# RMSNorm with swish on one core: regrouped loads and stores, a held first store, more row sums on ScalarE, and a small transfer ahead of gamma's

## The chip, the cores and the metric

The kernel runs on one NeuronCore of a Trainium2 chip. The metric is the device time of one launch in microseconds (us). A profiled execution also gives a span, from the first to the last instruction on the core.

## What is computed

The input `x` is 16 x 1024 x 512 in float32, that is 16384 rows of 512 numbers, 33.55 MB; the output has the same size. The reference, cut to what matters:

```python
rms = np.sqrt(np.mean(x ** 2, axis=-1, keepdims=True) + eps)
x_norm = x / rms * gamma
return x_norm * (1.0 / (1.0 + np.exp(-x_norm)))
```

So each row needs one sum of squares, one reciprocal square root, a product with gamma and the swish of the result.

## The kernel before, in words

**Tiles.** The 16384 rows are 128 per row of the tile, one or more for each of the 128 partitions. `sizes` cuts the 128 rows that each partition holds into 11 tiles of 4, 4, 8, six of 16, 8 and 8 rows. One row in one partition is 2 KB, so a tile of 16 rows is 4 MB, and in HBM each partition's part of it is one piece of 32 KB. `xb` is a ring of 96 rows in SBUF: tiles 0 to 7 fit without waiting, while the last three tiles overwrite the places of earlier ones and their loads wait until those are stored. Everything happens in place in `xb`.

**Loads.** All 11 loads are issued by SyncE (L118), the first two from the very start of the program. SyncE waits on the store's semaphore `st` where a load overwrites the ring.

**Units.** The work goes in 32 units of `cn` = 4 rows of each partition. For unit k:

- ScalarE, `square(k)`: waits for the tile's load at its first unit; one ACTIVATE squares the last row and adds it up into `ms` (L159, followed by a read of the accumulator); a second one squares the other three rows (`n_sq` = 3) into the PSUM buffer `sq[k % 2]` (L166), which waits for the sums of unit k - 2.
- VectorE, `sums(k)` (L204): one TENSOR_REDUCE of the three squared rows.
- GpSimd: adds eps (L141) and raises to -0.5 (L148), giving `rstd`.
- VectorE, `norm(k)` (L215): four SCALAR_TENSOR_TENSOR, one for each row, times `rstd` and gamma.
- ScalarE, `swish(k)` (L178): one ACTIVATE over the four rows.

**Order by hand.** Every engine takes its instructions in the written order. ScalarE: `square(k)`, then a store that has become due, then `swish(k - 2)`. VectorE: `sums(k)`, then `norm(k - 1)`. Once, between `sums(0)` and `sums(1)`, VectorE spreads gamma over the partitions with a STREAM_SHUFFLE (L228), which waits for gamma's load.

**Stores.** ScalarE issues them (L183) on its own DMA queue, each as soon as the last unit of its tile has its swish. The same queue carries gamma's load, 8 KB, as its first transfer (L187), after GpSimd has set `gamma4` to zero (L136). Gamma's load is followed on ScalarE by the load of the activation table (L190).

At the end SyncE waits for the stores that no load waited for. In the trace the queue q1 is SyncE's (loads) and q10 is ScalarE's (gamma and stores).

Of the kernel before, what the change touches and what calls it, by code (L numbers as in the profile page):

```python
# [8 lines left out]
@with_exitstack  # L9
def kernel(  # L10
    ctx: ExitStack,
    tc: tile.TileContext,
    x: bass.AP,
    gamma: bass.AP,
    eps: bass.AP,
    out: bass.AP,
):
    nc = tc.nc
    P = nc.NUM_PARTITIONS
    AF = mybir.ActivationFunctionType  # L20
    ALU = mybir.AluOpType
    fp32 = mybir.dt.float32
    bf16 = mybir.dt.bfloat16

    xf = x.flatten_outer_dims()
    of = out.flatten_outer_dims()
    R, D = xf.shape


    sizes = [4, 4, 8] + [16] * 6 + [8, 8]  # L30
    ring = 96
    early = 2
    cn = 4
    n_sq = 3
    N = sum(sizes)
    assert N * P == R, (N, R)


    tiles = []
    done = 0  # L40
    for sz in sizes:
        assert done % ring + sz <= ring
        tiles.append((done * P, sz, done % ring))
        done += sz
    T = len(tiles)

    chunks = [
        (t, r, r == at)
        for t, (_, sz, at) in enumerate(tiles)
        for r in range(at, at + sz, cn)  # L50
    ]
    K = len(chunks)
    ends = []
    e = 0
    for sz in sizes:
        e += sz // cn
        ends.append(e)

    inv_d = 1.0 / float(D)
    eps_f = float(eps)  # L60

    tc.close()
    tc.compile()  # L65

    def sbuf(name, shape, dt=fp32):
        return nc.alloc_sbuf_tensor(name, shape, dt).ap()

    xb = sbuf("xb", [P, ring, D])  # L70
    gamma4 = sbuf("gamma4", [P, D])
    gamma_sb = sbuf("gamma_sb", [P, D])
    junk = [sbuf(f"junk{i}", [P, D], bf16) for i in range(2)]
    neg_half = sbuf("neg_half", [P, cn])
    ms = sbuf("ms", [P, K, cn])
    aeps = sbuf("aeps", [P, K, cn])
    rstd = sbuf("rstd", [P, K, cn])
    sq = [nc.alloc_psum_tensor(f"sq{i}", [P, 4, D], fp32).ap() for i in range(2)]

    ld = [nc.alloc_semaphore(f"ld{t}") for t in range(T)]  # L80
    st = [nc.alloc_semaphore(f"st{t}") for t in range(T)]
    s_gld = nc.alloc_semaphore("s_gld")
    s_zero = nc.alloc_semaphore("s_zero")
    s_half = nc.alloc_semaphore("s_half")
    s_gamma = nc.alloc_semaphore("s_gamma")
    s_acc = nc.alloc_semaphore("s_acc")
    s_sq = nc.alloc_semaphore("s_sq")
    s_sum = nc.alloc_semaphore("s_sum")
    s_eps = nc.alloc_semaphore("s_eps")
    s_rstd = nc.alloc_semaphore("s_rstd")  # L90
    s_norm = nc.alloc_semaphore("s_norm")
    s_swish = nc.alloc_semaphore("s_swish")

    def need(ins, sem, value):
        return ins.wait_op(sem, value, "sem-ge")

    def dram(ap, t):
        first, sz, _ = tiles[t]
        return ap[first : first + P * sz].rearrange("(p n) d -> p n d", n=sz)

    def buf(t):
        _, sz, at = tiles[t]
        return xb[:, at : at + sz, :]


    stored_by_sync = set()

    def load(t):
        _, sz, at = tiles[t]
        waits = [  # L110
            u for u in range(t)
            if tiles[u][2] < at + sz and at < tiles[u][2] + tiles[u][1]
            and u not in stored_by_sync
        ]
        for u in waits:
            nc.sync.wait_ge(st[u], 16)
            stored_by_sync.add(u)
        return nc.sync.dma_start(out=buf(t), in_=dram(xf, t)).then_inc(ld[t], 16)  # L118

    entry = nc.main_func.blocks[0].instructions  # L120
    here = nc.cur_bb.bb.instructions
    for t in range(early):
        ins = load(t).ins
        assert here[-1] is ins or here[-1].name == ins.name
        here.pop()
        at = next(
            i for i, other in enumerate(entry)
            if other.engine == mybir.EngineType.SP
            and isinstance(other, mybir.InstDrain)
        )  # L130
        entry.insert(at, ins)
    for t in range(early, T):
        load(t)


    nc.gpsimd.memset(gamma4, 0.0).then_inc(s_zero, 1)  # L136
    nc.gpsimd.memset(neg_half, -0.5).then_inc(s_half, 1)  # L137
    nc.gpsimd.wait_ge(s_half, 1)
    for k in range(K):
        need(  # L140
            nc.gpsimd.tensor_scalar(  # L141
                out=aeps[:, k, :], in0=ms[:, k, :], scalar1=eps_f, scalar2=None,
                op0=ALU.add,
            ),
            s_sum, k + 1,
        ).then_inc(s_eps, 1)
        need(
            nc.gpsimd.tensor_tensor(  # L148
                out=rstd[:, k, :], in0=aeps[:, k, :], in1=neg_half, op=ALU.pow
            ),  # L150
            s_eps, k + 1,
        ).then_inc(s_rstd, 1)


    def square(k):
        t, at, first = chunks[k]
        if first:
            nc.scalar.wait_ge(ld[t], 16)  # L158
        acc = nc.scalar.activation(  # L159
            out=junk[k % 2], in_=xb[:, at + n_sq, :], func=AF.Square,  # L160
            scale=inv_d**0.5, accum_out=ms[:, k, n_sq : n_sq + 1],
        )
        if k >= 2:
            need(acc, s_acc, k - 1)
        acc.then_inc(s_acc, 1)
        square = nc.scalar.activation(  # L166
            out=sq[k % 2][:, 0:n_sq, :], in_=xb[:, at : at + n_sq, :],
            func=AF.Square, scale=inv_d**0.5,
        )
        if k >= 2:  # L170
            need(square, s_sum, k - 1)
        square.then_inc(s_sq, 1)

    def swish(k):
        _, at, _ = chunks[k]
        rows = xb[:, at : at + cn, :]
        need(
            nc.scalar.activation(out=rows, in_=rows, func=AF.Silu), s_norm, k + 1  # L178
        ).then_inc(s_swish, 1)

    def store(t):
        need(
            nc.scalar.dma_start(out=dram(of, t), in_=buf(t)), s_swish, ends[t]  # L183
        ).then_inc(st[t], 16)

    need(
        nc.scalar.dma_start(out=gamma4[0:P:32, :], in_=gamma.partition_broadcast(4)),  # L187
        s_zero, 1,
    ).then_inc(s_gld, 16)
    nc.scalar.preload_act_table_set("silu_and_others")  # L190
    stored = 0
    for k in range(K + 3):
        if k < K:
            square(k)
        while stored < T and ends[stored] <= k - 2:
            store(stored)
            stored += 1
        if 2 <= k < K + 2:
            swish(k - 2)


    def sums(k):
        need(
            nc.vector.tensor_reduce(  # L204
                out=ms[:, k, 0:n_sq], in_=sq[k % 2][:, 0:n_sq, :], op=ALU.add,
                axis=mybir.AxisListType.X,
            ),
            s_sq, k + 1,
        ).then_inc(s_sum, 1)

    def norm(k):
        _, at, _ = chunks[k]
        for j in range(cn):
            row = xb[:, at + j, :]
            ins = nc.vector.scalar_tensor_tensor(  # L215
                out=row, in0=row, scalar=rstd[:, k, j : j + 1], in1=gamma_sb,
                op0=ALU.mult, op1=ALU.mult,
            )
            if j == 0:
                need(ins, s_rstd, k + 1)  # L220
        ins.then_inc(s_norm, 1)

    for k in range(K + 1):
        if k < K:
            sums(k)
        if k == 0:
            need(
                nc.vector.stream_shuffle(gamma_sb, gamma4, [0] * 32), s_gld, 16  # L228
            ).then_inc(s_gamma, 1)
        if k == 1:  # L230
            nc.vector.wait_ge(s_gamma, 1)
        if k >= 1:
            norm(k - 1)


    for t in range(T):
        if t not in stored_by_sync:
            nc.sync.wait_ge(st[t], 16)

# [34 lines left out]
```

## Time and profile before

| what | value |
|---|---|
| median of 12 runs | 160.25 us (160.15 to 160.34) |
| the profiled execution's own time | 160.15 us |
| its span | 158.8 us |
| VectorE busy | 139.2 us (88% of the span) |
| ScalarE busy | 125.1 us (79%) |
| GpSimd busy | 85.1 us (54%) |
| bytes moved | 67.14 MB, mean 423 GB/s |
| loads, 11 DMAs from SyncE | issued from 0.0 to 80.5 us |
| stores, 11 DMAs from ScalarE | issued from 16.26 to 152.17 us |

How to read it: the profiled execution took 160.15 us, of which 158.8 us lie between the first and the last instruction and 1.35 us around them; it stands 0.10 us under the median. An engine's busy time leaves out the issuing of DMAs and waits. The 16 DMA engines have a row of their own in the page: their mean busy share and what they moved in each of 40 slices. A DMA is split over these engines by partition, eight partitions each, and the trace has one packet for each piece of contiguous bytes in one partition: 8 KB for a tile of 4 rows, 16 KB for 8, 32 KB for 16. A group's mean time in the page is that of one instruction including what overlaps the next one; the distance between two starts in the timeline is the cost in a queue that is full.

### The profile page before, as it was taken

Reading aid. Unit: us, or ns where it says so; the run is one execution under the profiler, and the core shown is the slowest. Engines: PE = TensorE matmul, PEld = TensorE weight load, DVE = VectorE, ACT = ScalarE, POOL = GpSimd, SP = SyncE. Lnnn points to the kernel's source line nnn. Section 1 sums busy time; section 2 is a strip of 40 time slices with the busy share of each in tenths; the row PEclk is TensorE's granted clock in tenths of the full one; section 3 lists DMA queues with packets and bytes.
Section 4 is the critical chain, followed back from the end, with each engine's and each line's share of the span. In section 5 each row is a group of like instructions: output and inputs, shape, how many; then the busy total and the mean of one; then the engine's idle time right before and its main releaser. Section 6 shows DMA issues by size and latency. Waiting matters only on the chain.

```text
span 158.8 us, 437 instructions
## 1 busy us (share of the span) xinstructions
DVE 139.2 (88%) x162; ACT 125.1 (79%) x129; POOL 85.1 (54%) x70
## 2 busy tenths in 40 slices
DVE  0298986999999999999999999999999999998600
ACT  1838839888888899888888888899888888883430
POOL 1043551445555554444444557888888888988100
DMA  7999989989999989999999999999999999999997
GB/s 248 435 508 396 396 363 485 448 378 462 390 452 413 487 375 489 404 404 479 429 413 406 495 413 404 425 437 462 400 458 404 446 425 454 429 421 446 396 404 330
DMA packets 3179, 67.14 MB, mean 423 GB/s; under 512 B 356, under 2 KB 356, under 8 KB 360
## 3 DMA queue, kind: packets, MB, share of 16 engines
q1 hardware_dynamic: 1584, 33.56, 49.9%
q10 hardware_dynamic: 1592, 33.56, 49.2%
q14 instruction: 3, 0.02, 0.0%
HBM read 33.56 MB, written 33.55 MB: 423 GB/s over the span
## 4 chain that ended last, share of the span: by engine, by line
DVE 76%; DMA 13%; ACT 2%; POOL 2%; issue 0%; SPq 0%; ACTq 0%
DVE xb L215 47%; DVE ms L204 29%; DMA xb<-in_x_dram 13%; POOL aeps L141 2%; ACT xb L178 1%; ACT sq L166 1%; POOL rstd L148 1%; ACT junk L159 0%; SPq L118 0%; ACTq L158 0%
## 5 line engine op out<-in xcount | busy, mean ns | idle before, releaser
L215 DVE SCALAR_TENSOR_TENSOR xb<-xb,rstd,gamma_sb 128x512 f32<-128x512 f32 x128 | 87.8, 759 | 1.2 <-POOL rstd L148 1.2
L141 POOL TENSOR_SCALAR aeps<-ms 128x4 f32<-128x4 f32 x32 | 44.5, 1390 | 58.0 <-DVE ms L204 58.0
L178 ACT ACTIVATE xb<-xb 128x2048 f32<-128x2048 f32 x32 | 61.1, 1908 | 17.6 <-DVE xb L215 17.6
L204 DVE TENSOR_REDUCE ms<-sq 128x3 f32<-128x1536 f32 x32 | 56.5, 1765 | 9.8 <-ACT sq L166 9.7
L166 ACT ACTIVATE sq<-xb 128x1536 f32<-128x1536 f32 x32 | 45.9, 1434 | 0.0
L148 POOL TENSOR_TENSOR rstd<-aeps,neg_half 128x4 f32<-128x4 f32 x32 | 39.8, 1245 | 2.7
L159 ACT ACTIVATE junk<-xb 128x512 bf16<-128x512 f32 x32 | 19.7, 615 | 5.8 <-DMA xb<-in_x_dram 5.8
L159 ACT ACTIVATION_READ_ACCUMULATOR junk<-xb 128x1 f32 x32 | 6.0, 187 | 0.0
L190 ACT ACT_TABLE_LOAD x1 | 1.3, 1283 | 3.6 <-issue 3.6
L136 POOL MEMSET gamma<- 128x512 f32 x1 | 0.5, 524 | 1.5 <-POOLq L65 1.5
L228 DVE STREAM_SHUFFLE gamma_sb<-gamma 128x512 f32<-128x512 f32 x1 | 0.7, 720 | 0.0
L255 POOL MEMSET const-float32-0.0<- 128x1 f32 x1 | 0.1, 98 | 0.2 <-issue 0.2
L255 POOL MEMSET const-uint8-127<- 128x1 uint8 x1 | 0.1, 102 | 0.0
L255 POOL MEMSET const-bfloat16-1.0<- 128x1 bf16 x1 | 0.1, 101 | 0.0
L137 POOL MEMSET neg_half<- 128x4 f32 x1 | 0.1, 101 | 0.0
L255 POOL MEMSET const-float32-1.0<- 128x1 f32 x1 | 0.1, 98 | 0.0
L228 DVE LOAD_MASK_SELECT gamma_sb<-gamma x1 | 0.0, 14 | 0.0
## 6 DMA issues: line engine op xcount, KB each, us to landing
xb<-in_x_dram SPq DMA_DIRECT2D x6, 4096.0 KB, 43.5
out_dram<-xb ACTq DMA_DIRECT2D x6, 4096.0 KB, 29.8
xb<-in_x_dram SPq DMA_DIRECT2D x3, 2048.0 KB, 37.2
out_dram<-xb ACTq DMA_DIRECT2D x3, 2048.0 KB, 10.1
xb<-in_x_dram SPq DMA_DIRECT2D x2, 1024.0 KB, 5.9
out_dram<-xb ACTq DMA_DIRECT2D x2, 1024.0 KB, 19.5
gamma<-in_gamma_dram ACTq DMA_DIRECT2D x1, 8.0 KB
```

The source lines that it names most:

```text
L136: nc.gpsimd.memset(gamma4, 0.0).then_inc(s_zero, 1)
L137: nc.gpsimd.memset(neg_half, -0.5).then_inc(s_half, 1)
L141: nc.gpsimd.tensor_scalar(out=aeps[:, k, :], in0=ms[:, k, :], scalar1=eps_f, scalar2=None, op0=ALU.add,),
L148: nc.gpsimd.tensor_tensor(out=rstd[:, k, :], in0=aeps[:, k, :], in1=neg_half, op=ALU.pow),
L159: acc = nc.scalar.activation(out=junk[k % 2], in_=xb[:, at + n_sq, :], func=AF.Square, scale=inv_d**0.5, accum_out=ms[:, k, n_sq : n_sq + 1],)
L166: square = nc.scalar.activation(out=sq[k % 2][:, 0:n_sq, :], in_=xb[:, at : at + n_sq, :], func=AF.Square, scale=inv_d**0.5,)
L178: nc.scalar.activation(out=rows, in_=rows, func=AF.Silu), s_norm, k + 1
L190: nc.scalar.preload_act_table_set("silu_and_others")
L204: nc.vector.tensor_reduce(out=ms[:, k, 0:n_sq], in_=sq[k % 2][:, 0:n_sq, :], op=ALU.add, axis=mybir.AxisListType.X,),
L215: ins = nc.vector.scalar_tensor_tensor(out=row, in0=row, scalar=rstd[:, k, j : j + 1], in1=gamma_sb, op0=ALU.mult, op1=ALU.mult,)
L228: nc.vector.stream_shuffle(gamma_sb, gamma4, [0] * 32), s_gld, 16
L255: nc = _bacc.Bacc("TRN2", target_bir_lowering=False, num_devices=1)
```

## The change

Four things change together.

1. **A transfer of 8 KB out.** GpSimd first sets a tile `blank` of 128 x 16 floats to zero; ScalarE issues a DMA from it to a scratch tensor in HBM, ahead of gamma's on the same queue. It consists of 128 pieces of 64 bytes. SyncE waits for its end after its last load.
2. **Groups, loads and stores.** The tiles are replaced by five groups of 16, 48, 32, 16 and 16 rows, each contiguous in HBM. Loads and stores are pieces of a group. There are 8 loads in place of 11, two of them of 32 rows (64 KB in a partition), and 8 stores in place of 11, one of them of 32 rows. A load waits for whichever stores cover the rows that it overwrites: the load of group 3 for the store of group 0, the load of group 4 for the store of 32 rows.
3. **Held stores.** No store is issued before `square(8)` has been; before, the first one followed `square(3)`.
4. **Two row sums on ScalarE.** In every third unit (k % 3 == 2, ten units of the 32) ScalarE sums two rows with its accumulator and squares two for VectorE's reduction, in place of one and three. The accumulator's throw-away output alternates by row, with a semaphore for each buffer.

The loops of VectorE, of ScalarE and of GpSimd keep their order otherwise. The diff, cut to its core:

```diff
-    sizes = [4, 4, 8] + [16] * 6 + [8, 8]
+    groups = [16, 48, 32, 16, 16]
     ring = 96
+    loads = [(0, 0, 4), (0, 4, 4), (0, 8, 8), (1, 0, 16), (1, 16, 32), (2, 0, 32),
+        (3, 0, 16), (4, 0, 16)]
+    stores = [(0, 0, 16), (1, 0, 32), (1, 32, 16), (2, 0, 16), (2, 16, 16), (3, 0, 16),
+        (4, 0, 8), (4, 8, 8)]
-    n_sq = 3
+    held = 8
+    def n_sq(k):
+        return 2 if k % 3 == 2 else 3
...
+    ends = [-(-(begin[g] + r + n) // cn) for g, r, n in stores]
...
+    scratch = nc.dram_tensor("scratch", [P, 16], fp32, kind="Internal").ap()
+    blank = sbuf("blank", [P, 16])
...
     def dram(ap, piece):
+        g, r, n = piece
+        rows = ap[begin[g] * P : (begin[g] + groups[g]) * P]
+        return rows.rearrange("(p n) d -> p n d", n=groups[g])[:, r : r + n, :]
...
+    nc.sync.wait_ge(s_scratch, 16)
+    nc.gpsimd.memset(blank, 0.0).then_inc(s_blank, 1)
     nc.gpsimd.memset(gamma4, 0.0).then_inc(s_zero, 1)
...
     def square(k):
-        if first:
-            nc.scalar.wait_ge(ld[t], 16)
+        at, landing = chunks[k]
+        for i in landing:
+            nc.scalar.wait_ge(ld[i], 16)
+        n = n_sq(k)
+        for j in range(n, cn):
+            acc = nc.scalar.activation(
+                out=junk[j % 2], in_=xb[:, at + j, :], func=AF.Square,
+                scale=inv_d**0.5, accum_out=ms[:, k, j : j + 1],
+            )
...
+    need(nc.scalar.dma_start(out=scratch, in_=blank), s_blank, 1).then_inc(
+        s_scratch, 16
+    )
     need(
         nc.scalar.dma_start(out=gamma4[0:P:32, :], in_=gamma.partition_broadcast(4)),
         s_zero, 1,
     ).then_inc(s_gld, 16)
...
-        while stored < T and ends[stored] <= k - 2:
+        while k >= held and stored < len(stores) and ends[stored] <= k - 2:
             store(stored)
             stored += 1
...
-                out=ms[:, k, 0:n_sq], in_=sq[k % 2][:, 0:n_sq, :], op=ALU.add,
+                out=ms[:, k, 0 : n_sq(k)], in_=sq[k % 2][:, 0 : n_sq(k), :], op=ALU.add,
```

## The prediction

> **What bounds the kernel now.** I read the page first: engines, DMA row, queues.
>
> ```profile
> DVE 139.2 (88%) x162; ACT 125.1 (79%) x129; POOL 85.1 (54%) x70
> ...
> DMA  7999989989999989999999999999999999999997
> ...
> q1 hardware_dynamic: 1584, 33.56, 49.9%
> q10 hardware_dynamic: 1592, 33.56, 49.2%
> ```
>
> The two queues together use 99.1% of 16 engines' span: 157.4 of 158.8 us. The DMA engines are full from the first packet (0.99 us) to the last slice. The chain of waits nevertheless shows VectorE:
>
> ```profile
> 137.59 1.67 DVE ms L204
> 139.26 2.65 DVE xb L215 x4
> 141.91 1.68 DVE ms L204
> ...
> 147.46 2.75 DVE xb L215 x4
> 150.21 0.02 issue
> 150.23 1.91 ACT xb L178
> ```
>
> One unit costs VectorE 1.67 + 2.65 = 4.32 us, without a gap from unit 4 on. Both are true: the last store is issued at 152.17, its first packet starts at 153.01, and by the packet records the store ahead of it ends at 153.6. Compute is 0.6 us earlier than the DMA engines need it. The kernel is balanced, so a gain on one side alone is worth nothing. The timeline of one late unit shows ScalarE's part:
>
> ```profile
> 139.44 0.61 ACT L159 ACTIVATE junk<-xb 128x512 bf16<-128x512 f32 x1
> 140.05 1.43 ACT L166 ACTIVATE sq<-xb 128x1536 f32<-128x1536 f32 x1
> 141.78 1.79 DVE L204 TENSOR_REDUCE ms<-sq 128x3 f32<-128x1536 f32 x1
> 141.94 1.91 ACT L178 ACTIVATE xb<-xb 128x2048 f32<-128x2048 f32 x1 [0.45 <-DVE xb L215]
> ```
>
> The squares are ready at 141.48, 0.30 us before VectorE takes them: ScalarE has little room either.
>
> [...] with stores of 8 KB against loads of 32 KB the stores get 23% of the packet time from 20 to 24 us, near 8/(8+32). [...] Here a 32 KB packet takes 1213 ns, so 16 engines reach 432. Nothing in the change lifts that. [...] In the trace the eps addition takes 0.66 us up to 91.9 us and 2.65 us, the length of a norm, from 96.2 us on.
>
> **Part 1, fewer and longer packets.** Packets of 8, 16 and 32 KB take 309, 611 and 1213 ns: 2 x 309 - 611 = 7 and 2 x 611 - 1213 = 9, so about 8 ns for each packet beside its bytes. 22 DMAs with 8 packets per engine become 16: 48 fewer, -0.38 us; six completion packets of 9 ns less, -0.05. If rows of 64 KB travel as two packets, 24 of the 48 come back and the gain is 0.2. The rows of a group now lie 32 to 96 KB apart; I price that at nothing, as no row of before shows a cost.
>
> **Part 2, the scratch transfer.** Eight packets of 64 bytes per engine, unknown here: at least the 9 ns of a 4-byte packet, at most the 84 ns that gamma's 2 KB took, 0.07 to 0.67 us. I take 0.25. Besides, the first store has a price in before: from 18.8 us on, loads of 1213 ns took up to 1871, about 0.5 us on each engine, some 2.5 us after that store's issue:
>
> ```profile
> 16.00:20.00 4.00, 4.00 (x6) 3.31 (x5) 2.04 (x2) 1.00 1.03 393
> 20.00:42.00 22.00, 19.84 (x25) 17.97 (x20) 10.00 (x10) 1.00 0.99 423
> 42.00:70.00 28.00, 28.00 (x32) 24.83 (x26) 12.49 (x13) 1.00 1.01 435
> ```
>
> (Third to last column is the clock, then DMA share and GB/s: 393 against 435.) If it is a first write's cost, scratch pays it at 4 to 7 us instead; the engines are full there too, so it moves and is not saved: 0, with -0.5 as the other end. SP's added wait stands behind its last load and holds nothing up. On ScalarE the issue of gamma, the table load and unit 0 are queued behind scratch's: a first issue took 1.09 us (gamma, in before), a later one 0.34, so unit 0 starts at most 0.4 later than 4.87. The waits for loads ahead of units 1 and 2, 0.43 and 2.91 us, cover that; without them it would cost 0.4. GpSimd's added memset, 0.1 us, delays gamma's by as much.
>
> Gamma is behind scratch, and VectorE's shuffle behind gamma:
>
> ```profile
> 2.45 1.09 ACTq L187 DMA_DIRECT2D gamma<-in_gamma_dram  x1
> ...
> 8.65 0.72 DVE L228 STREAM_SHUFFLE gamma_sb<-gamma 128x512 f32<-128x512 f32 x1
> 9.45 1.76 DVE L204 TENSOR_REDUCE ms<-sq 128x3 f32<-128x1536 f32 x1
> ```
>
> Gamma's packet started at 7.42 and its completion was recorded at 8.58, just in time. Scratch is issued about 0.4 us earlier (it waits for the shorter memset), so its first packet starts near 6.5 to 7. Then packets alternate with the loads' 16 KB ones: eight times 0.62 us, then scratch's completion, gamma, gamma's completion, some of them between 1.2 us packets. Gamma lands at 12.4 to 14.1 us, middle 13.2. VectorE then starts unit 1's sums 0.87 us later, at 14.1 (before: 9.45). Queued behind it are all sums and norms, and ScalarE's swishes after those.
>
> **Part 3, held stores and the 32-row load.** Load 3 ended at 22.46 with stores taking 0.45 us of that; without them 22.0. The next 32 rows per partition take 16 x 1.21 = 19.4, so they end at 41.4, seen by ScalarE 0.6 later (as with load 3: 22.46 and 23.13), at 42.0. Units 8 to 15 now all wait for that load. `square(8)` is 2 x 0.61 + 1.02 us (613 ns for 512 elements and 1434 for 1536 make 1.02 us for 1024), so sums(8) begins at 44.2, against 42.57 before: a stall of 1.6 us, hidden only because compute is faster later. Gamma's delay hides in the same stall up to a point: from sums(1) to sums(8) are 29.7 us (five periods of 4.32, two of 4.05, below), so gamma may land as late as 44.2 - 29.7 - 0.87 = 13.6 us.
>
> **Part 4, two row sums.** VectorE's reduction of two rows: it loses at most a third of 1.67, 0.56; [...] I take 1.13 and a period of 3.78; no row of before has this shape. But the next unit's squares come first: swish(k-2) starts 0.16 after sums(k), takes 1.82, then 0.61 + 1.43 + 0.03 for three rows: 4.05. So ten units save 0.27 us each, not 0.53. Slow GpSimd gives the same bound: rstd comes 1.21 us after the norm, 0.1 later than a reduction of 1.13. ScalarE's own extra 0.61 - 0.41 = 0.20 in the two-row unit fits in its 0.30 of room. From sums(8) to sums(31): 23 x 4.32 = 99.3, less 0.5 for the period after the stall (ScalarE is ahead there) and 7 x 0.27: 96.9. sums(31) at 141.1 instead of 141.78, last store at 151.5 instead of 152.17. That serves the DMA engines, which are due about 0.2 us earlier.
>
> **Is the DMA kept full?** By 70.4 us the engines have done the 96 rows of the ring and group 0's store (22.0 + 38.7 + 9.7). Group 3's load needs that store. Store 1 (32 rows) goes out after `square(14)`: 44.2 + 25.1 - 0.1, with 0.84 to its first packet at 70.0. Margin 0.4 us, and only that. After it stores and loads overlap amply: group 4's load lands near 120 to 124, unit 28 needs it near 126.
>
> **Sum.** -0.38 - 0.05 + 0.25 = -0.2 us on a full DMA: span 158.6, execution 159.95; the median is 0.10 higher: 160.05.
>
> **Rivals.**
> - *Gamma late* (33%). One mechanism: 64-byte packets each wait out a load's packet, gamma lands after 13.6 us, sums(8) is late by the excess, store 1 misses its 0.4 us and the DMA engines run dry near 70 us. At 15 us: 1.4 late, 1.0 dry, 160.05 + 1.0 = 161.0, slower. For: gamma's own completion packet waited 0.6 us for a load's packet. Against: the middle is 13.2, below the point that decides.
> - *First write's pause gone* (15%): 0.5 us saved, 159.5. For: it occurs once in before. Against: there is no idle DMA time to hide it in.
> - *Rows of 64 KB are cut* (12%): the change does not lengthen packets. Store 0 gets half of the engines, ends near 66 us, no hole; 160.2.
> - My forecast, all full and gamma in time: 40%.
>
> **Chances.** 0.2% (0.32 us) is about what a measurement of this kernel can tell from no change. Forecast's own range 159.8 to 160.4: of its 40%, 15 fall under 159.93, 25 within. Cut rows: 11 within, 1 above. Pause gone: 15 faster. Gamma late: 33 slower. Faster 0.30, same 0.36, slower 0.34. Range 159.4 to 161.4, which leaves out the ends of the pause case and of the late one.
>
> **What would show it.** DMA share at 9 in every slice; sums(8) near 44.2 after a wait for the load; periods of 4.32, 4.32, 4.05; the shuffle at 13.2; the last store's issue near 151.5. Wrong if a DMA slice near 70 us drops, if two-row periods reach 3.8, if packets slow down with the wider rows, or if the shuffle comes after 13.6.

## The result and the profile after

The changed kernel takes 163.76 us (median of 8 runs, 163.34 to 164.27) against 160.28 us for the kernel before, measured beside it (32 runs). The ratio is 1.0214, with a 95% interval from 1.0202 to 1.0226: slower by 3.5 us. The forecast was 160.05 with a range up to 161.4, so the time lies outside it. The profiled execution has a span of 162.5 us, 3.9 more than the forecast's 158.6.

The page of the changed kernel, its lines on engines, the DMA row, the rate and the two queues:

```profile
span 162.5 us, 449 instructions
...
DVE 134.5 (83%) x162; ACT 126.5 (78%) x149; POOL 65.5 (40%) x71
...
DMA  7999998999999999996999979999999999999981
GB/s 268 439 458 403 492 524 371 403 516 419 355 389 389 411 468 403 460 548 282 478 403 403 581 298 371 460 427 395 476 411 403 484 403 419 468 403 423 415 343 60
...
q1 hardware_dynamic: 1152, 33.55, 49.0%
q10 hardware_dynamic: 1304, 33.57, 48.1%
```

VectorE has 4.7 us less work, as intended. The DMA row is full up to the last two slices, and the last slice moves 60 GB/s in place of 330 in the kernel before. The same stretches of time at the end of both kernels; the columns after the engines are clock, DMA share and GB/s. The changed kernel:

```profile
124.00:154.00 30.00, 23.29 (x29) 20.53 (x21) 10.22 (x10) 1.00 0.99 427
154.00:158.00 4.00, 0.00 (x0) 0.00 (x0) 0.00 (x0) 1.00 0.87 373
158.00:162.50 4.50, 0.00 (x0) 0.00 (x0) 0.00 (x0) 1.00 0.14 58
```

And the kernel before:

```profile
124.00:154.00 30.00, 24.96 (x30) 21.41 (x20) 20.18 (x12) 1.00 0.98 423
154.00:158.00 4.00, 0.00 (x0) 0.00 (x0) 0.00 (x0) 1.00 0.95 406
158.00:158.80 0.80, 0.00 (x0) 0.00 (x0) 0.00 (x0) 1.00 0.01 0
```

The compute is over before 154 us in both. What is new is a tail of 4 us in which the DMA engines are used to 14%: a few of the 16 are still at work and the rest have nothing left. I sorted the packets of the trace into 16 sequences, each packet behind the one that ended closest before its start; every sequence then holds about 4.19 MB, so some must have been slower. "Over" is the time of its packets beyond the usual one for their size (309, 611, 1213 and, for 64 KB, 2418 ns); a packet with such extra time is called stretched below. Where two engines end within a few ns of each other the sorting can swap them, so one figure can be off by some 0.3 us:

```
                        end of the sequence, us          over, us
before,  16 engines     157.9 to 158.5                   1.0 to 2.2
changed, 13 engines     157.5 to 158.1                   1.3 to 2.2
changed, engine A       160.95                           4.7
changed, engine B       161.69                           5.3
changed, engine C       162.14                           5.3

over by stretch of 10 us, starting at    50    60    70    80    90   100   110
engine A                               0.00  0.00  0.10  0.96  1.80  0.16  0.16
engine B                               0.56  0.16  0.51  0.48  0.85  0.87  0.53
engine C                               0.01  0.00  0.84  1.34  0.67  0.82  0.52
any of the other 13, at most           0.00  0.00  0.14  0.23  0.30  0.01  0.06
```

Thirteen engines end as early as in the kernel before. Three lose 3 us or more beyond the others, all of it between 50 and 120 us. A little over half of these three engines' extra time in that stretch, some 6.3 us of 11.4 in all, lies in packets of 64 KB, which take up to 3.26 us in place of 2.42. The rest, about 5 us, lies in loads of 32 KB that run on the same engines beside the 64 KB store or within 20 us after it, up to 2.19 us in place of 1.21. The last store's completion on its 16 engines is spread over 4.59 us, against 0.48 before. From 20 to 40 us, when 64 KB packets only come in and nothing goes out, no packet is stretched; nor, but for less than 0.1 us on any engine, after 124 us, when packets of at most 32 KB only go out.

The chain of waits of the changed kernel, four of its last pieces, leads over the same transfers:

```profile
66.46 34.78 DMA out_dram<-xb
...
101.25 24.87 DMA xb<-in_x_dram
...
142.71 5.31 DVE xb L241 x8
...
148.04 1.91 ACT xb L200
```

The 34.78 us are the store of 32 rows. By the completion records its fast engines were done at 97.1, its slowest at 101.2; only then could the load of the last group start.

### The profile page after: what moved, and what is told of

It is laid out like the page before. It is cut to its first block, busy times and chain, and to the rows that moved or that the text cites. A ratio compares the mean times of both kernels' runs of the same rounds, so it can differ in the third digit from the quotient of the medians.

```text
span 162.5 us, 449 instructions
## 1 busy us (share of the span) xinstructions
DVE 134.5 (83%) x162; ACT 126.5 (78%) x149; POOL 65.5 (40%) x71
## 4 chain that ended last, share of the span: by engine, by line
DMA 60%; DVE 20%; ACT 10%; SPq 0%; issue 0%; ACTq 0%
DMA xb<-in_x_dram 39%; DMA out_dram<-xb 21%; DVE xb L241 13%; DVE ms L230 7%; ACT xb L200 5%; ACT sq L188 3%; ACT junk L179 2%; SPq L130 0%; ACTq L176 0%
## 5 line engine op out<-in xcount | busy, mean ns | idle before, releaser
L230 DVE TENSOR_REDUCE ms<-sq 128x3 f32<-128x1536 f32 (+1 forms) x32 | 50.8, 1587 | 11.0 <-ACT sq L188 9.7
L157 POOL TENSOR_SCALAR aeps<-ms 128x4 f32<-128x4 f32 x32 | 20.6, 644 | 75.1 <-DVE ms L230 75.1
L164 POOL TENSOR_TENSOR rstd<-aeps,neg_half 128x4 f32<-128x4 f32 x32 | 44.0, 1376 | 2.7
L188 ACT ACTIVATE sq<-xb 128x1536 f32<-128x1536 f32 (+1 forms) x32 | 41.6, 1299 | 0.0
L179 ACT ACTIVATE junk<-xb 128x512 bf16<-128x512 f32 x42 | 25.8, 616 | 6.7 <-DMA xb<-in_x_dram 6.6
L179 ACT ACTIVATION_READ_ACCUMULATOR junk<-xb 128x1 f32 x42 | 7.8, 187 | 0.0
## 6 DMA issues: line engine op xcount, KB each, us to landing
xb<-in_x_dram SPq DMA_DIRECT2D x1, 2048.0 KB, 10.4
```

What stands on the lines that cost most here:

```text
L157: nc.gpsimd.tensor_scalar(out=aeps[:, k, :], in0=ms[:, k, :], scalar1=eps_f, scalar2=None, op0=ALU.add,),
L164: nc.gpsimd.tensor_tensor(out=rstd[:, k, :], in0=aeps[:, k, :], in1=neg_half, op=ALU.pow),
L179: acc = nc.scalar.activation(out=junk[j % 2], in_=xb[:, at + j, :], func=AF.Square, scale=inv_d**0.5, accum_out=ms[:, k, j : j + 1],)
L188: square = nc.scalar.activation(out=sq[k % 2][:, 0:n, :], in_=xb[:, at : at + n, :], func=AF.Square, scale=inv_d**0.5,)
L230: nc.vector.tensor_reduce(out=ms[:, k, 0 : n_sq(k)], in_=sq[k % 2][:, 0 : n_sq(k), :], op=ALU.add, axis=mybir.AxisListType.X,),
```

## The experiments

The theory after the result: **P**, long packets (64 KB) of the store, beside loads, slow some engines, and the slowest engine sets the end. Rivals: **L**, the long packets of the loads do it; **W**, the pitch of 96 KB between rows of the 48-row group. Each ratio below is to the kernel before, run beside it on the same chip.

### Cutting the 32-row store, the 32-row loads, both

```diff
-    stores = [(0, 0, 16), (1, 0, 32), (1, 32, 16), ...
+    stores = [(0, 0, 16), (1, 0, 16), (1, 16, 16), (1, 32, 16), ...
```

> The changed kernel with its one store of 32 rows (64 KB packets) cut into two stores of 16 rows; loads, groups, held stores, scratch and row sums stay. In the changed kernel three DMA engines end 3.4 to 4.6 us after the other thirteen; they fall behind between 72 and 118 us, while stores of 64 KB run beside loads. Theory P (long store packets beside loads slow some engines): the lag goes, 160.0 to 160.6. Theory L (long load packets do it): the lag stays in part or whole, 162 to 164. Theory W (the pitch of 96 KB between rows of the 48-row group in HBM, whatever the packet): 163 to 164.

Measured: 161.78 us, ratio 1.009 (1.0069 to 1.011). In its profile two engines end 1.3 us after the middle of the others, and all 16 together lose about 0.6 us between 80 and 90 us.

```diff
-    loads = [..., (1, 16, 32), (2, 0, 32), (3, 0, 16), (4, 0, 16)]
+    loads = [..., (1, 16, 16), (1, 32, 16), (2, 0, 16), (2, 16, 16), (3, 0, 16), (4, 0, 16)]
```

> The changed kernel with its two loads of 32 rows cut into four of 16; the 32-row store stays. Theory P: three engines still fall behind while the 64 KB stores run, 163 to 164. Theory L: the lag goes, 160.0 to 160.6. Theory W: 163 to 164. In all of them the wait of unit 8 for a 32-row load goes: sums(8) near 41.5 in place of 43.65.

Measured: 160.88 us, ratio 1.0057 (1.0033 to 1.0082), with runs from 160.42 to 162.98. Four or five engines end about 1.1 us late. In this profile the 64 KB stores themselves are stretched by only 0.3 us in all; the late engines lost their time in packets of 32 KB, at 52 to 61 us and near 96 us. sums(8) begins at 41.04, as expected of a unit that no longer waits.

> The changed kernel with both cut: no packet over 32 KB, the groups of 48 and 32 rows stay. Theories P and L: 160.0 to 160.6. Theory W: 163 to 164, with some engines behind. If compute is then ahead and the DMA full, about 160.2.

Measured: 160.28 us, ratio 0.9999 (0.999 to 1.0008). The engines end within 1.1 us of each other. So W falls: the groups and their pitch are still there. P and L as I had put them fall too: of the 3.5 us, cutting the store takes 2.0 and cutting the loads 2.9, and neither takes all. What the times leave is P': this kernel loses as long as packets of 64 KB run on either queue (2.1% with both, 0.9% with the loads alone, 0.6% with the store alone). It speaks of what removes the loss; by the profiles the lost time itself lies in 64 KB packets and in 32 KB ones. The same kernel shows something else. Its DMA row and its last units:

```profile
DMA  7999999999799999999999999999999999999996
```

```profile
138.31 1.75 DVE L230 TENSOR_REDUCE ms<-sq 128x3 f32<-128x1536 f32 x1
...
147.33 0.34 ACTq L205 DMA_DIRECT2D out_dram<-xb  x1
```

VectorE's last sums begin 3.5 us earlier than before (141.78) and the last store is issued 4.8 us earlier (152.17), and the time is the same to 0.1%. The DMA engines had no use for it.

### Without the scratch transfer

```diff
-    need(nc.scalar.dma_start(out=scratch, in_=blank), s_blank, 1).then_inc(s_scratch, 16)
-    nc.sync.wait_ge(s_scratch, 16)
-    nc.gpsimd.memset(blank, 0.0).then_inc(s_blank, 1)
```

> The changed kernel without the 8 KB transfer to scratch, its wait and its memset. Theories P, L and W: 163.3 to 164.0, no difference over 0.3 us from the changed kernel, only gamma's shuffle back near 8.6 from 11.2 us and the pause at the first store (16 packets, 0.7 us each, at 43 us) as before. If scratch is part of the loss: under 162.

Measured: 163.17 us, ratio 1.0186 (1.0162 to 1.0209), which overlaps the changed kernel's; it is 0.1 us under the range expected. Three engines end 3 us late here too. Without scratch 2.9 us of the loss are still there, so scratch can be at most a small part of it. The pause at the first store is 1.7 us on each engine in this profile and 0.7 in the changed kernel's; one profile of each does not make that a rule.

### Long transfers made of short packets

```diff
-        rows = ap[begin[g] * P : (begin[g] + groups[g]) * P]
-        return rows.rearrange("(p n) d -> p n d", n=groups[g])[:, r : r + n, :]
+        m = min(n, 16)
+        rows = ap[(begin[g] + r) * P : (begin[g] + r + n) * P]
+        return rows.rearrange("(c p n) d -> p c n d", n=m, p=P)
...
```

The SBUF side is split in two in the same way. The transfers and waits stay those of the changed kernel; a 32-row transfer is now two packets of 32 KB in each partition. Rows of the first and the last group come out in another order, because their loads and stores cut them differently; the traffic is the same.

> The changed kernel with the same loads, stores and waits, two loads and one store of 32 rows among them, but with the rows dealt out so that a 32-row transfer is two pieces of 32 KB in each partition: no packet over 32 KB. Theory P (the 64 KB packet itself): the lag of some engines goes, 160.1 to 160.7, with unit 8 still waiting to about 43.6 us. Rival D (the long DMA and what waits for it, whatever its packets): 161.5 to 164.

Measured: 160.47 us, ratio 1.0009 (0.9991 to 1.0027), with single runs up to 162.1. Unit 8 still waits for the 32-row load:

```profile
43.64 1.23 DVE L231 TENSOR_REDUCE ms<-sq 128x2 f32<-128x1024 f32 x1 [2.45 <-ACT sq L189]
```

The stall of unit 8 is as in the changed kernel (43.65), and with it every long wait, yet the loss is gone (160.47 against the changed kernel's 163.76). So what counts here is the length of the packet, not that of the transfer. The edit also changes where the rows lie in HBM, but the kernel with both cut has the places of the changed kernel and no loss either. A profiled run of 161.01 us has one engine 1 us late, so packets of 32 KB are not free of it altogether.

### The kernel before with 64 KB rows

```diff
-    sizes = [4, 4, 8] + [16] * 6 + [8, 8]
+    sizes = [4, 4, 8, 16, 32, 32, 16, 8, 8]
```

> The kernel before with tiles of 4, 4, 8, 16, 32, 32, 16, 8 and 8 rows, so two loads and two stores of 64 KB rows, each tile contiguous in HBM; early stores, no scratch, three rows reduced on VectorE. Theory P: some engines fall behind by 2 to 5 us, 162 to 165. Rival H (it takes the held stores or the scratch): 160.2 to 161 plus what waiting for a 32-row tile costs compute.

Measured: 163.92 us, ratio 1.0226 (1.0205 to 1.0246). The number is the one that P wanted, and the reason is another. All 16 engines end together here (161.99 to 162.17). Two did stretch by 2.3 us more than the rest, but near 120 us nearly all stand still:

```profile
DMA  7999999696969698799999988979939599699997
```

```profile
122.22 0.34 ACTq L183 DMA_DIRECT2D out_dram<-xb  x1
```

By 122.1 the last load had landed, and the store of the second 32-row tile could go out only after its eight units, at 122.22: some 4 us of idle DMA. So the time doesn't decide between P and H. The packets say something, though: two engines were stretched without held stores and without scratch, so the stretching needs neither. The run also shows a second price of large tiles, which the changed kernel avoids by storing that stretch in pieces of 16 rows.

### The traffic alone

```diff
-    ... (gamma and the units of all engines)
+    for t in range(T):
+        nc.scalar.wait_ge(ld[t], 16)
+        nc.scalar.dma_start(out=dram(of, t), in_=buf(t)).then_inc(st[t], 16)
```

`sizes` is eight tiles of 16 rows in one copy, four of 32 in the other.

> A copy of x to the output through the same ring with tiles of 16 rows and no computation (the norm and the swish are left out, gamma is not loaded). The DMA alone: 67.1 MB in packets of 1213 ns are 155.2 us of 16 engines; with about 1 us before the first packet and 1.35 outside the span, 158 to 159. The engines end within 1.5 us of each other.

Measured: 159.94 us, ratio 0.9965 (0.995 to 0.9981), 1 us above the range expected. The engines end within 1.0 us of each other.

> The same copy with four tiles of 32 rows, packets of 64 KB. Theory P, if DMA traffic alone suffices: some engines end 2 us or more after the others, 160 to 164. Rival E (packets stretch only where the compute engines use SBUF at the same time): within 0.5 us of the copy with 32 KB packets, up to 2 us more for the first store's later start if the queues run dry.

Measured: 162.62 us, ratio 1.0118 (1.0092 to 1.0143), from 160.53 to 163.06. The profiled run was the one of 160.53, and shows no lag; the other eleven lie at 161.91 or above. So it was run again.

> The copy with packets of 64 KB once more, for a profile of a usual run: the profile there is of the fastest of its twelve runs (160.53 against a median of 162.62) and shows no lag (again no norm and no swish). Theory P: a run near 162.6 with some engines 2 us or more behind the others and their packets stretched. Rival G (all engines stand still together, between transfers): all end together, with over 2 us of idle DMA time.

Measured: one run of 159.91 us, on another chip, without a lag. That left the question open, and three kernels were put side by side on a further chip.

> The changed kernel once more, beside the two copies on one chip. If the lag of some engines belongs to 64 KB packets wherever they run: 163 to 164.3, with two to four engines 3 us or more behind at the end. Rival C (the lag belongs to some chips): the time can lie anywhere from 160 to 164, and the copy with 64 KB packets moves with it.

Measured: 163.92 us, ratio 1.0226 (1.0196 to 1.0256); two engines end at 161.7 and 162.2, the others by 158.0.

> The copy with 64 KB packets (no norm, no swish, no gamma), beside the changed kernel. Theory P with traffic alone: 161.5 to 163, some engines behind, their packets stretched. Rival E (it takes the compute beside it, or the first wait of the queues): 159.9 to 160.5 while the changed kernel is at 163 or more.

Measured: 162.58 us, ratio 1.0145 (1.0117 to 1.0173).

> The copy with 32 KB packets (no norm, no swish, no gamma) on the same chip, as the floor: 159.6 to 160.2, engines within 1.2 us of each other, in every theory.

Measured: 160.11 us, ratio 0.9982 (0.9969 to 0.9994).

The stretches of time of the copy with 64 KB packets; ahead of the clock stands only GpSimd, which does nothing:

```profile
130.00:144.00 14.00, 0.00 (x0) 1.00 0.89 384
144.00:158.00 14.00, 0.00 (x0) 1.00 1.03 445
158.00:161.10 3.10, 0.00 (x0) 1.00 0.05 21
```

And of the copy with 32 KB packets:

```profile
130.00:144.00 14.00, 0.00 (x0) 1.00 0.99 426
144.00:158.00 14.00, 0.00 (x0) 1.00 0.96 414
158.00:159.00 1.00, 0.00 (x0) 1.00 0.00 0
```

With 64 KB two of the sixteen sequences are over by 2.0 and 1.2 us between 110 and 130 us, where loads and stores alternate, and no other by more than 0.2. Those two hold up the fourth and last load (landed on the first engine at 136.1, on the last at 139.3), and the other engines wait up to 2 us for the last store: the 0.89. With 32 KB no packet from 20 us to the end is stretched. The loss with 64 KB packets is there with no computation beside it, and rival E falls. Rival C is not excluded: the changed kernel lost 3.5 and 3.6 us in its two measurements, but the single run of the 64 KB copy on the other chip had no lag. The chip alone cannot be the answer, since on one chip eleven runs of that copy were slow and one was not.

### The other parts alone, on the kernel before

The two row sums (the diff is cut to its core):

```diff
-        acc = nc.scalar.activation(out=junk[k % 2], in_=xb[:, at + n_sq, :], ...)
+        n = n_sq(k)
+        for j in range(n, cn):
+            acc = nc.scalar.activation(out=junk[j % 2], in_=xb[:, at + j, :], ...)
```

> The kernel before with the two row sums on ScalarE in every third unit and nothing else changed. Theory P with the DMA as the floor: VectorE's last sums begin near 139 instead of 141.78 us, the last store is issued 2 us or more earlier, and the time moves by no more than 0.2 us, 160.0 to 160.3. Rival V (VectorE bounds the kernel): 2 to 3 us faster, 157.5 to 158.5.

Measured: 160.27 us, ratio 0.9999 (0.9983 to 1.0015).

```profile
138.86 1.75 DVE L212 TENSOR_REDUCE ms<-sq 128x3 f32<-128x1536 f32 x1
...
147.88 0.34 ACTq L191 DMA_DIRECT2D out_dram<-xb  x1
```

2.9 us earlier on VectorE and 4.3 at the last store are worth nothing: rival V falls.

Scratch alone (the lines of the change, put into the kernel before):

> The kernel before with the 8 KB transfer to scratch ahead of gamma's and nothing else. Gamma lands near 11 us instead of 8.6 and VectorE's units 1 to 4 begin later. Stated as the prediction had it: 160.2 to 160.8 (+0.1 to +0.6, mostly compute that comes later, since the kernel before has only 0.6 us of room at its end). Rival S (scratch takes away the pause at the first store): 159.7 to 160.0.

Measured: 160.20 us, ratio 0.999 (0.9975 to 1.0006).

```profile
11.03 0.72 DVE L237 STREAM_SHUFFLE gamma_sb<-gamma 128x512 f32<-128x512 f32 x1
11.64 1.74 DVE L213 TENSOR_REDUCE ms<-sq 128x3 f32<-128x1536 f32 x1
```

Gamma comes 2.4 us later and costs nothing that can be measured; the last store is even issued at 150.09, 2.1 us earlier than before. The packets' time beyond the usual is 1.49 us per engine here and 1.52 before, so it is not less with scratch, and S isn't shown either.

Held stores alone:

```diff
-        while stored < T and ends[stored] <= k - 2:
+        while k >= 8 and stored < T and ends[stored] <= k - 2:
```

> The kernel before with no store until square(8) has been issued. If the queues stay full: 160.1 to 160.4. Rival: the ring's later loads come late and the DMA engines run dry or compute waits, 160.8 or more.

Measured: 160.49 us, ratio 1.0008 (0.9991 to 1.0026): no difference that can be told.

No version beat the kernel before beyond its interval except the bare copy, which does no work; it leaves 0.2 to 0.4% to win with packets of 32 KB.

## Why the prediction was wrong, by its steps

**The DMA as the bound**: right. With both cut, with the long transfers in short packets and with the row sums alone, the last store is issued 2.9 to 4.8 us earlier than before, and the time is the same.

**Part 1, fewer and longer packets**: this is the step that failed. I priced a longer packet at its bytes plus 8 ns and said -0.38 us. Of the 384 packets of 64 KB, 338 do take that to within 20 ns, 2418 ns in the median, and without the extra time of the stretched ones the DMA time fell by 0.35 us per engine (157.41 - 1.52 before, 157.79 - 2.25 after). But the sum divided the work by 16 engines as if all packets of a size took the same time and the engines ended together. With 64 KB packets three engines lose 3 us and more on stretched packets, and the end is theirs: the span grew by 3.7 us (158.8 to 162.5) where the sum had -0.2. Why those packets stretch stays open. The prediction named "if packets slow down with the wider rows" among what would make it wrong, and gave it no case, no chance and no part of the range.

**The pitch of the rows at nothing**: right (both cuts together, 160.28).

**Part 2, scratch**: its 64-byte packets take 11 ns, 0.09 us per engine, near the lower bound of 0.07. Gamma landed at 11.16 us, earlier than 12.4 to 14.1: scratch's first packet started at 5.6, not 6.5 to 7, 3.5 us after its issue at 2.04, where gamma's in the kernel before came 5.0 us after. The issue took 0.34 us, and gamma's behind it still 1.08, so the 1.09 of before was gamma's and not that of a first issue. The packets alternate with the loads' one for one, as the prediction took it: on one engine they mostly start 0.31 us apart while the loads' packets are of 8 KB and 0.61 us apart once they are of 16 KB, and they run from 5.6 to 9.2 us. The rival *gamma late* did not come about. The pause at the first store is still there (0.7 us per engine near 43 us). So the 0 in the sum was near, but by luck: the reason given, that scratch would take the pause over, is not what happened.

**Part 3**: sums(8) at 43.65 for 44.2; right in kind and nearly in size. The rival *rows of 64 KB are cut* is excluded: the trace has 384 packets of 65536 bytes.

**The DMA kept full near 70 us**: it was; from 64 to 80 us the packets' times fill all 16 engines. Store 1 was issued at 66.46, not 69.2: it went out as soon as the swish it needs had ended (66.43), while `square(14)` was still running. Its first packet followed at 70.12, behind store 0.

**Part 4**: a reduction of two rows takes 1.14 us from start to start (forecast 1.13, which was my estimate) and the period after it 4.01 (4.05), bound by ScalarE's swish and squares:

```profile
56.07 1.22 DVE L230 TENSOR_REDUCE ms<-sq 128x2 f32<-128x1024 f32 x1
56.19 1.91 ACT L200 ACTIVATE xb<-xb 128x2048 f32<-128x2048 f32 x1 [0.27 <-DVE xb L241]
...
60.08 1.76 DVE L230 TENSOR_REDUCE ms<-sq 128x3 f32<-128x1536 f32 x1
```

sums(31) began at 140.96 (141.1). The last store was issued at 149.98 (151.5); the forecast took the 10.4 us between the two from the kernel before, with eps additions of 2.65 us, while here GpSimd's stayed at 0.66 us to the end, which it did not foresee; what made them slow in the kernel before is not shown. The compute of the changed kernel is as good as forecast; it only isn't what ends last.

## What to carry to other kernels

Here the DMA engines were full from end to end (99.1% of the span in the kernel before), and shortening an engine's work or issuing a store 2.9 to 4.8 us earlier bought nothing that could be told. In such a kernel measure the bare copy with the same traffic first; here it leaves 0.2 to 0.4%. Do not count DMA time as bytes over 16 engines: look at the completion times of one transfer on all its engines, since what waits for it waits for the slowest (here the store of 32 rows was done at 97.1 us on the first engine and at 101.2 on the last). With loads and stores together, packets of 32 KB were safer here than 64 KB (160.28 against 163.76 us), and the longer transfers could be had without longer packets (160.47).

## What the runs showed of the hardware that was not expected

- With loads and stores alternating and packets of 64 KB among them, some packets are stretched on two or three engines of the 16 and much less on the others: in the changed kernel 64 KB ones up to 3.26 us in place of 2.42, and 32 KB loads up to 2.19 in place of 1.21. There this adds up to 3.2 to 4.2 us on three engines between 50 and 120 us, in the bare copy to 2.0 and 1.2 us on two between 110 and 130 us. What in an engine or in memory does it, and why two profiled runs of the bare copy, on two chips, were free of it, stays open.
- Around the first packet of the first large store, packets are stretched by 0.2 to 1.7 us per engine in the mean of the 16, in all 17 profiles here, the bare copies too. With scratch, a small store, ahead of it the changed kernel still has 0.7 us. Its cause stays open.
